# Sparse attention in a two-block transformer kernel: other places for weight splits, PSUM temporaries, and another order of attention units

## The chip, the cores and the metric

The kernel runs on one core of a Trainium2 chip. The time is the device time of one execution in microseconds (us); lower is better. The engines are TensorE (PE, with PEld for its weight loads), VectorE (DVE), ScalarE (ACT) and GpSimd (POOL); SyncE (SP) issues the weight DMAs. Each engine runs its instructions in program order.

## The reference

Two transformer blocks on 256 tokens of width 1024. The first has a convolution and neighbourhood attention, then a mixture of 16 experts. The second has sparse attention (DSA), an MLP, latent attention (MLA) and another MLP. The change lies in the sparse attention:

```python
score = einsum('bqh,bqhs->bqs', wib * 8**-0.5, relu(einsum('bqhd,bsd->bqhs', qib, ki) * 64**-0.5))
score = where(admiss, score, NEG)
_, idx = lax.top_k(score, n_top)              # n_top = 64 of up to 256 keys
logits = q . k[idx] * 64**-0.5 + bias[idx]    # 16 heads of 64; q and k RMS-normalised
out = (softmax(where(valid, logits, NEG)) @ v[idx]) @ w_o
```

## The kernel before, in words

The program is written in a manual order: each engine takes its instructions in the order in which the Python code emits them. Weights come by DMA from SyncE through a ring of buffers (`take`, `free`, `pump`); a buffer is loaded again when both halves in it have been freed.

*Splits.* The large products of this part run as three fp32r matmuls (`mm3`: high·high, low·high, high·low). Each 128x2048 weight tile is split by `split`: ScalarE copies the high half (L330), then VectorE (L334) or GpSimd (L332) subtracts to get the low half. The splits are numbered: 0 to 3 are the projections of k, index q, index k and v (`kvi`), 4 to 7 the four q projections (`qproj`), 8 to 11 the output projection (`WO.slot`), 12 and on the MLP. The set `on_dve` (L1092) says which low halves are VectorE's; the others are GpSimd's. `wahead(k)` emits the splits up to number k - 1 where it stands in the program, and `wnext(la)` hands out the next one after emitting `la` more ahead.

*Index.* For two tiles of 128 queries (qt = 0, 1; tile 1 sees 256 keys, tile 0 sees 128) `index_mm` makes the scores of 8 heads, `index_acc` accumulates them with per-row weights on VectorE (L1386, L1388, L1390), and `index_top` finds the 64 largest by 8 rounds of max and match-replace (L1398, L1399) and writes a mask (L1400). Before that, the row scales `rr` come from column sums by a chain of small VectorE instructions, the last eight of them in `rsq` (L288 to L295, a reciprocal square root from an integer guess and two refinements), and are broadcast by TensorE into a PSUM bank `rb_`.

*Query scales.* `qstat` sums the squares of q on TensorE, and `qscale(g)` turns the sums of 8 heads into scales, again by `rsq`.

*Attention.* It works on 8 units (qt, u) of 4 heads. `pipeline` emits for i = -2, -1, 0, ...: the scores S(i+2) (`dsa_score`, two PSUM banks of tag A, the mask added by a matmul with `idr`), the finished output fin(i-2) (`hilo_v`, L346 and L347), the normalisation of unit i (reciprocals L1254 on VectorE, the product L1255 on GpSimd), the softmax of unit i+1 (`dsa_soft`: sums L1479 and negated maxima L1482 on VectorE, exponentials L1484 on ScalarE), the functions in `pre[i]`, the values PV(i-1), the transposes T(i) (L1265, copied by ScalarE, L1268), and the functions in `hooks[i]`. In the call, the first dictionary is `hooks`, the second `pre`.

Four PSUM banks of tag A and four of tag B go round; a bank is written again when its last reader is done.

## Time and profile before

| | us |
|---|---|
| median of 3 runs | 1748.01 (1747.1 to 1751.78) |
| profiled execution, device time | 1741.9 |
| its span, first to last instruction | 1740.1 |

| engine | busy us | share of the span | instructions |
|---|---|---|---|
| PE | 1356.5 | 78% | 9581 |
| PEld | 873.8 | 50% | 9581 |
| DVE | 542.5 | 31% | 1037 |
| ACT | 426.0 | 24% | 649 |
| POOL | 271.8 | 16% | 124 |

The shares are averages over stages: up to about 1110 us the experts' weights stream in, and the chain of waits is DMA; from there on it is engines. The index and the sparse attention lie between about 1150 and 1251 us. The mean granted TensorE clock is 0.885. In timeline rows, a start and a length in us stand in front, and brackets at the end give the idle time before the instruction and what ended it.

### The profile page before, as it was taken

How to read it: one execution, taken by the hardware profiler on the slowest of the kernel's cores; microseconds unless marked ns; L12 is line 12 of the kernel's file. 1: busy time of each engine (PE TensorE's matmuls, PEld its weight loads, DVE VectorE, ACT ScalarE, POOL GpSimd, SP SyncE). 2: the span in 40 equal slices, each digit the busy share in tenths (PEclk: the TensorE clock that was granted, in tenths of full speed). 3: DMA queues.
4: the chain of work that ended last, by engine and by line, in shares of the span. 5: the costliest groups of instructions: out<-in, count | busy, mean ns of one | idle time of the engine just before them, and what ended most of it. 6: DMA issues, size and time to landing. Idle time of an engine off the chain costs nothing.

```text
span 1740.1 us, 22284 instructions
## 1 busy us (share of the span) xinstructions
PE 1356.5 (78%) x9581; PEld 873.8 (50%) x9581; DVE 542.5 (31%) x1037; ACT 426.0 (24%) x649; POOL 271.8 (16%) x124
## 2 busy tenths in 40 slices
PE   6899987666666655665666656798999999999998
PEld 3775842111111111221111111385899999889998
DVE  3885321000000000000000000278653457756434
ACT  3434510000000000000000000254554446455442
POOL 2521210000000000000000000152335221323531
PEclk9999999868778878878788787798999999999999
DMA  9649779999999999999999999972255544225450
GB/s 397 240 156 417 290 326 429 427 428 428 427 428 428 427 428 427 427 429 427 428 427 428 428 428 428 399 287 97 97 194 194 194 174 154 97 98 194 178 201 34
DMA packets 59475, 545.85 MB, mean 314 GB/s; under 512 B 5552, under 2 KB 9008, under 8 KB 26032
## 3 DMA queue, kind: packets, MB, share of 16 engines
q1 hardware_dynamic: 56400, 537.71, 74.9%
q10 hardware_dynamic: 2976, 6.72, 1.1%
q8 instruction: 75, 1.23, 0.3%
q14 instruction: 24, 0.20, 0.0%
HBM read 543.36 MB, written 1.05 MB: 313 GB/s over the span
## 4 chain that ended last, share of the span: by engine, by line
DMA 52%; PE 38%; DVE 5%; ACT 3%; issue 2%; POOL 1%; ACTq 0%; SPq 0%; DVEq 0%; POOLq 0%
DMA moe__w<-in_w_gu_dram 32%; DMA moe__w<-in_w_dn_dram 15%; PE mlp__psB L94 10%; PE mlp__psA L94 9%; PE index__psA L94 2%; DMA moe__w<-in_w_dl_dram 2%; PE mlaproj__psA L94 1%; PE mlawo__psA L94 1%; PE qkv__psA L94 1%; PE qkv__psB L94 1%; PE uproj__psA L94 1%; PE moe__psB L94 1%; DMA na__nb<-in_nab_dram 1%; PE router__psB L94 1%; PE wout__psA L94 1%
## 5 line engine op out<-in xcount | busy, mean ns | idle before, releaser
L94 PE MATMUL moe__psB<-moe__w,moe__xsT 128*32 128x512 f32 x1920 | 304.0, 767 | 191.7 <-DMA moe__w<-in_w_gu_dram 191.6
L94 PEld LDWEIGHTS moe__psB<-moe__w,moe__xsT 128*32 128x32 f32 x1920 | 58.9, 126 | 422.9 <-DMA moe__w<-in_w_gu_dram 312.3
L94 PE MATMUL moe__psB<-moe__w,moe__hT 128*32 128x512 f32 (+1 forms) x984 | 167.5, 808 | 103.1 <-DMA moe__w<-in_w_dn_dram 94.1
L1134 DVE TENSOR_TENSOR moe__hid<-moe__hid,moe__psB 128x512 f32<-128x512 f32 x15 | 10.3, 687 | 555.8 <-PE moe__psB L94 555.8
L332 POOL TENSOR_TENSOR dsaproj__wl<-moe__w,dsaproj__wh 128x1680 fp32r<-128x1680 f32 (+1 forms) x5 | 19.7, 3945 | 908.9 <-ACT dsaproj__wh L330 902.2
L94 PEld LDWEIGHTS moe__psB<-moe__w,moe__hT 128*32 128x32 f32 x984 | 38.4, 133 | 214.9 <-DMA moe__w<-in_w_dn_dram 139.7
L94 PE MATMUL mlp__psA<-mlp__hh,mlp__wl 128*128 128x256 f32 x512 | 141.3, 276 | 0.0
L94 PE MATMUL mlp__psA<-mlp__hh,mlp__wh 128*128 128x256 f32 x512 | 141.3, 276 | 0.0
L94 PE MATMUL mlp__psA<-mlp__hl,mlp__wh 128*128 128x256 f32 x512 | 141.3, 276 | 0.0
L1133 ACT ACTIVATE moe__hid<-moe__psB 128x512 f32<-128x512 f32 x15 | 9.0, 597 | 537.8 <-PE moe__psB L94 537.8
L94 PE MATMUL mlp__psB<-mlp__xgh,mlp__wh 128*128 128x256 f32 x448 | 123.8, 276 | 0.0
L94 PE MATMUL mlp__psB<-mlp__xgh,mlp__wl 128*128 128x256 f32 x448 | 123.7, 276 | 0.0
L94 PE MATMUL mlp__psB<-mlp__xgl,mlp__wh 128*128 128x256 f32 x448 | 123.7, 276 | 0.0
L330 ACT ACTIVATE mlp__wh<-mlp__w 128x2048 fp32r<-128x2048 f32 (+1 forms) x51 | 96.8, 1900 | 62.3 <-PE mlp__psA L94 48.6
L334 DVE TENSOR_TENSOR mlp__wl<-mlp__w,mlp__wh 128x2048 fp32r<-128x2048 f32 (+1 forms) x35 | 84.7, 2420 | 80.1 <-ACT mlp__wh L330 80.1
L332 POOL TENSOR_TENSOR mlp__wl<-mlp__w,mlp__wh 128x2048 fp32r<-128x2048 f32 x16 | 74.4, 4648 | 147.5 <-ACT mlp__wh L330 147.5
L94 PEld LDWEIGHTS mlp__psA<-mlp__hh,mlp__wh 128*128 128x128 f32 x512 | 96.1, 188 | 0.0
L94 PEld LDWEIGHTS mlp__psA<-mlp__hl,mlp__wh 128*128 128x128 f32 x512 | 96.1, 188 | 0.0
L94 PEld LDWEIGHTS mlp__psA<-mlp__hh,mlp__wl 128*128 128x128 f32 x512 | 96.1, 188 | 0.0
L1169 DVE COPY moe__ys<-moe__psB 128x512 f32<-128x512 f32 x15 | 10.4, 691 | 243.7 <-PE moe__psB L94 243.7
L94 PEld LDWEIGHTS mlp__psB<-mlp__xgh,mlp__wl 128*128 128x128 f32 x448 | 84.1, 188 | 0.0
L94 PEld LDWEIGHTS mlp__psB<-mlp__xgl,mlp__wh 128*128 128x128 f32 x448 | 84.1, 188 | 0.0
(602 smaller groups left out, 2508.2 us busy)
## 6 DMA issues: line engine op xcount, KB each, us to landing
moe__w<-in_w_gu_dram SPq DMA_DIRECT2D x120, 2048.0 KB, 39.1
moe__w<-in_w_dn_dram SPq DMA_DIRECT2D x57, 2048.0 KB, 39.1
mlp__w<-in_mlp_down_dram SPq DMA_DIRECT2D x28, 1024.0 KB, 7.0
mlp__w<-in_mlp_up_dram SPq DMA_DIRECT2D x20, 1024.0 KB, 4.9
qkv__w<-in_w_mod_dram SPq DMA_DIRECT2D x12, 1024.0 KB, 7.0
start__w<-in_w_mod_dram SPq DMA_DIRECT2D x8, 1024.0 KB, 13.5
mod__w<-in_w_gu_dram SPq DMA_DIRECT2D x4, 2048.0 KB, 20.8
wout__w<-in_w_gu_dram SPq DMA_DIRECT2D x4, 2048.0 KB, 8.4
```

The costliest lines, as they stand in the source:

```text
L94: nc.tensor.matmul(o, lhsT, rhs, start=start, stop=stop, skip_group_check=True)
L330: nc.scalar.activation(h[:, 0:n], f, AF.Copy)
L332: nc.gpsimd.tensor_tensor(out=l[:, 0:n], in0=f, in1=h[:, 0:n].bitcast(F32), op=ALU.subtract)
L334: nc.vector.tensor_tensor(out=l[:, 0:n], in0=f, in1=h[:, 0:n].bitcast(F32), op=ALU.subtract)
L1133: nc.scalar.activation(hid, gp, AF.Silu)
L1134: nc.vector.tensor_mul(hid, hid, up)
L1169: nc.vector.tensor_copy(ys[1], yp[1])
```

## The change

The low halves of splits 7 and 9 go from GpSimd to VectorE. Split 5 moves from the end of `kvi` to a place in front of the accumulation of query tile 1; split 6 from in front of the first q projection to behind it; split 7 to behind the accumulation of tile 0; splits 8 and 9 from in front of the attention into it (`pre[2]`, `pre[3]`). A new helper `rsq_p` keeps half of its temporaries, and its input, in PSUM. The row sums, their products and the query sums stay in their PSUM banks. The accumulation of tile 1 reads the broadcast scale from PSUM. The identity's cast goes from GpSimd to ScalarE. The softmax adds and takes its maxima in the score bank, and the exponentials read that bank. The units' order is new, and the second top-k (`itop`) stands one hook behind the second query scale instead of in front of it.

```diff
+    def rsq_p(pool_, v, n, tag, ps):
+        r, r1, out_ = (small(pool_, n, tag + k) for k in "012")
+        t = small(pool_, n, "rq_t")
+        a, b = ps[:, 0:n], ps[:, n:2 * n]
+        nc.vector.tensor_scalar(r.bitcast(I32), v.bitcast(I32), -0.5, 1597463007.0, ALU.mult, ALU.add)
+        nc.vector.tensor_tensor(out=a, in0=v, in1=r, op=ALU.mult)
+        nc.vector.tensor_tensor(out=t, in0=a, in1=r, op=ALU.mult)
+        nc.vector.scalar_tensor_tensor(out=b, in0=t, scalar=-10.0 / 3.0, in1=t, op0=ALU.add, op1=ALU.mult)
+        nc.vector.scalar_tensor_tensor(out=r1, in0=b, scalar=5.0, in1=r, op0=ALU.add, op1=ALU.mult)
+        nc.vector.scalar_tensor_tensor(out=a, in0=v, scalar=-27.0 / 1024.0, in1=r1, op0=ALU.mult, op1=ALU.mult)
+        nc.vector.tensor_tensor(out=b, in0=a, in1=r1, op=ALU.mult)
+        nc.vector.scalar_tensor_tensor(out=out_, in0=b, scalar=0.5625, in1=r1, op0=ALU.add, op1=ALU.mult)
+        return out_
...
-        on_dve = {5, 8, 10, 11} | {n for n in range(12, 90) if n % 3 or 43 < n < 54}
+        on_dve = {5, 7, 8, 9, 10, 11} | {n for n in range(12, 90) if n % 3 or 43 < n < 54}
...
-                w = wnext(2 if s == 3 else 0)
+                w = wnext(1 if s == 3 else 0)
...
-        vr = cols[:, 0:4]
-        v1, pv, iv1, v2c, ep, ipv = (cols[:, 2 * i:2 * i + 2] for i in range(6))
+        v1, iv1, ep = (cols[:, 2 * i:2 * i + 2] for i in range(3))
+        vr = sps[:, 32:36]
+        vp1, pv, v2c, ipv = (sps[:, 32 + 2 * i:34 + 2 * i] for i in range(4))
...
-        nc.gpsimd.tensor_copy(idr, ident)
...
+        nc.vector.tensor_scalar(vp1, sps[:, 0:2], 1.0 / D, EPS, ALU.mult, ALU.add)
...
-        rr = rsq(pa, vr, 4, "rr")
+        rr = rsq_p(pa, vr, 4, "rr", sps[:, 64:72])
...
         def qproj(u):
-            w = wnext()
+            w = wnext(0)
...
-            vq = small(pool_, 16, "vq")
+            vq = qc[:, 32:48]
...
-            rqq = rsq(pool_, vq, 16, "rqq")
+            rqq = rsq_p(pool_, vq, 16, "rqq", qc[:, 64:96])
...
-            nc.vector.tensor_tensor(out=sc[:, 0:nk], in0=sc[:, 0:nk], in1=r12b[:, 0:nk], op=ALU.mult)
+            nc.vector.tensor_tensor(out=sc[:, 0:nk], in0=sc[:, 0:nk], in1=r12[:, 0:nk], op=ALU.mult)
...
-        rk = rsq(pa, vk, 2, "rk")
-        scs[1] = index_acc(1, rl1)
+        rk = rsq_p(pa, vk, 2, "rk", kst[:, 16:20])
+        wahead(6)
+        scs[1] = index_acc(1, rl1, rb_)
         rl0 = index_mm(0)
         nc.scalar.activation(r1b, rb_[:, T:2 * T], AF.Copy)
+        nc.scalar.activation(idr, ident, AF.Copy)
         qproj(0)
+        wahead(7)
         index_top(1, scs[1])
...
-        scs[0] = index_acc(0, rl0)
+        scs[0] = index_acc(0, rl0, r12b)
+        wahead(8)
         qproj(1)
         qstat(0)
         qproj(2)
         qstat(1)
-        wahead(10)
...
+                psv = pss[par][:, 0:2 * nk].rearrange("p (a k) -> p a k", a=2)
...
-                    nc.vector.scalar_tensor_tensor(out=s[:, a, 0:nk], in0=pss[par][:, a * nk:(a + 1) * nk],
-                                                   scalar=rq[:, qt, hd:hd + 1], in1=bm[:, 2 * par + a, :],
-                                                   op0=ALU.mult, op1=ALU.add)
-                nc.vector.tensor_reduce(nmx, s[:, :, 0:nk], axis=AX.X, op=ALU.max, negate=True)
+                    nc.vector.scalar_tensor_tensor(out=psv[:, a, :], in0=psv[:, a, :], scalar=rq[:, qt, hd:hd + 1],
+                                                   in1=bm[:, 2 * par + a, :], op0=ALU.mult, op1=ALU.add)
+                nc.vector.tensor_reduce(nmx, psv, axis=AX.X, op=ALU.max, negate=True)
...
-                    nc.scalar.activation(s[:, a, 0:nk], s[:, a, 0:nk], AF.Exp, bias=nmx[:, a:a + 1],
+                    nc.scalar.activation(s[:, a, 0:nk], psv[:, a, :], AF.Exp, bias=nmx[:, a:a + 1],
...
-                  [(1, 0), (1, 1), (1, 2), (0, 0), (0, 1), (1, 3), (0, 2), (0, 3)])
+                  [(1, 0), (1, 1), (1, 2), (1, 3), (0, 0), (0, 1), (0, 2), (0, 3)])
...
-        pipeline(att, 8, "dsaatt", {-2: [lambda: qscale(0, pb)], -1: [q_last, itop], 0: [q_last2], 8: [wo.slot(2, (1,))]},
-                 {6: [wo.slot(0), x3(range(0, 3))], 7: [wo.slot(1), x3(range(3, 6))],
+        pipeline(att, 8, "dsaatt", {-2: [lambda: qscale(0, pb)], -1: [q_last], 0: [q_last2], 1: [itop], 8: [wo.slot(2, (1,))]},
+                 {2: [lambda: wahead(9)], 3: [lambda: wahead(10)], 6: [wo.slot(0), x3(range(0, 3))], 7: [wo.slot(1), x3(range(3, 6))],
```

## Rows read from the trace of the kernel before

**Rows 1.** Chain of waits, 1149 to 1256 us: start us, us, what.

```profile
1173.71 5.66 PE index__psA L94 x48
...
1189.81 8.05 PE index__psA L94 x48
...
1198.81 1.73 PE dsaatt__psA L94 x10
...
1224.28 6.11 PE dsawo__psA L94 x48
...
1231.40 0.60 PE dsaatt__psB L1265 x4
```

**Rows 2.** Windows: engines' busy us (xcount), granted TensorE clock, DMA share, GB/s.

```profile
1188.80:1205.50 16.70, 14.95 (x94) 11.85 (x94) 13.96 (x55) 6.56 (x20) 2.04 (x2) 0.82 0.30 122
1205.50:1224.00 18.50, 15.41 (x97) 10.04 (x97) 16.20 (x51) 12.55 (x45) 8.48 (x10) 0.86 0.00 1
1224.00:1251.00 27.00, 26.80 (x219) 24.65 (x217) 15.88 (x31) 12.28 (x20) 9.11 (x5) 0.97 0.25 84
```

**Rows 3.** VectorE timeline, 1149 to 1181: start us, us, instruction, [idle before, releaser].

```profile
1149.68 4.97 DVE L334 TENSOR_TENSOR dsaproj__wl<-moe__w,dsaproj__wh 128x2048 fp32r<-128x2048 f32 x1 [3.18 <-ACT dsaproj__wh L330]
...
1159.77 0.35 DVE L1386 TENSOR_SCALAR index__sc<-index__rl,dsaproj__wi 128x256 f32<-128x256 f32 x1
...
1172.62 1.95 DVE L1400 TENSOR_SCALAR dsaproj__msk<-index__sc 128x256 fp32r<-128x256 f32 x1
...
1180.39 0.41 DVE L1351 COPY dsaatt__rw<-index__psB 8x256 f32<-8x256 f32 x1
```

**Rows 4.** GpSimd timeline, 1147 to 1188 us.

```profile
1147.92 4.58 POOL L332 TENSOR_TENSOR dsaproj__wl<-moe__w,dsaproj__wh 128x2048 fp32r<-128x2048 f32 x1 [3.44 <-PE dsaproj__psB L94]
...
1169.83 4.59 POOL L332 TENSOR_TENSOR index__wl<-dsaproj__w,index__wh 128x2048 fp32r<-128x2048 f32 x1 [0.84 <-ACT index__wh L330]
...
1182.54 4.51 POOL L332 TENSOR_TENSOR index__wl<-dsaproj__w,index__wh 128x2048 fp32r<-128x2048 f32 x1 [8.12 <-ACT index__wh L330]
```

**Rows 5.** TensorE timeline, the broadcast of the row scales.

```profile
1157.14 2.00 PE L94 MATMUL index__psA<-cst,dsaproj__rr 128*128 128x128 f32 x8 [3.52 <-DVE dsaproj__rr L295]
```

**Rows 6.** ScalarE timeline, 1159 to 1230 us.

```profile
1159.18 0.38 ACT L1416 ACTIVATE dsaproj__r12b<-index__psA 128x256 f32<-128x256 f32 x1 [5.13 <-PE index__psA L94]
...
1191.32 0.19 ACT L1484 ACTIVATION_READ_ACCUMULATOR dsaatt__ss<-dsaatt__ss,dsaatt__nmx 128x1 f32 x1
...
1198.52 0.63 ACT L1338 ACTIVATE index__sq<-dsaproj__qs 128x512 f32<-128x512 f32 x1
...
1227.51 1.90 ACT L330 ACTIVATE dsawo__wh<-dsaproj__w 128x2048 fp32r<-128x2048 f32 x1
```

**Rows 7.** VectorE timeline, 1182 to 1206 us.

```profile
1182.70 4.37 DVE L288 TENSOR_SCALAR dsaatt__rqq<-dsaatt__vq 128x16 int32<-128x16 int32 x1
...
1188.78 0.88 DVE L1479 SCALAR_TENSOR_TENSOR dsaatt__ss<-dsaatt__psA,dsaproj__rq,dsaproj__t 128x256 f32<-128x256 f32 x2
...
1197.72 0.23 DVE L1400 TENSOR_SCALAR dsaproj__msk<-index__sc 128x128 fp32r<-128x128 f32 x1
...
1202.41 0.41 DVE L1351 COPY index__rw<-index__psB 8x256 f32<-8x256 f32 x1 [1.33 <-PE index__psB L94]
...
1205.49 0.86 DVE L1479 SCALAR_TENSOR_TENSOR dsaatt__ss<-dsaatt__psA,dsaproj__rq,dsaproj__t 128x256 f32<-128x256 f32 x2
```

**Rows 8.** VectorE timeline, 1208 to 1233 us.

```profile
1208.50 0.42 DVE L346 CAST index__mixah<-dsaatt__psB 128x256 fp32r<-128x256 f32 x1
...
1224.34 0.59 DVE L1479 SCALAR_TENSOR_TENSOR dsaatt__ss<-dsaatt__psA,dsaproj__rq,dsaproj__t 128x128 f32<-128x128 f32 x2
...
1229.45 2.29 DVE L334 TENSOR_TENSOR dsawo__wl<-dsaproj__w,dsawo__wh 128x2048 fp32r<-128x2048 f32 x1 [3.09 <-ACT dsawo__wh L330]
...
1231.65 1.27 DVE L1503 SCALAR_TENSOR_TENSOR x<-x,vec,dsaproj__r1b 128x256 f32<-128x256 f32 x3
```

**Rows 9.** VectorE group by line and shape, whole span: busy us, mean ns.

```profile
L670 DVE SCALAR_TENSOR_TENSOR conv__psA<-rms__vp,vec,conv__psA 128x256 f32<-128x256 f32 x120 | 58.8, 490 | 4.1
```

More of the change, by code (lines that the diff above doesn't have):

```diff
@@ L1379, in index_mm, with index_acc @@
             return rls
-        def index_acc(qt, rls):
+        def index_acc(qt, rls, r12):
             nk = P * (qt + 1)
@@ L1416 @@
         nc.scalar.activation(r12b, rb_[:, 0:T], AF.Copy)
-        vk = small(pa, 2, "vk")
+        vk = kst[:, 8:10]
         nc.vector.scalar_tensor_tensor(out=vk, in0=kst[:, 0:2], scalar=1.0 / 64, in1=ep, op0=ALU.mult, op1=ALU.add)
-        rk = rsq(pa, vk, 2, "rk")
-        scs[1] = index_acc(1, rl1)
+        rk = rsq_p(pa, vk, 2, "rk", kst[:, 16:20])
+        wahead(6)
+        scs[1] = index_acc(1, rl1, rb_)
         rl0 = index_mm(0)
         nc.scalar.activation(r1b, rb_[:, T:2 * T], AF.Copy)
+        nc.scalar.activation(idr, ident, AF.Copy)
         qproj(0)
+        wahead(7)
         index_top(1, scs[1])
```

## The prediction

> **What bounds the kernel now.** I read the chain of waits first, then the windows, then the timelines of single engines. The chain shows that from 1149 to 1251 us several engines take turns in setting the end: the q projections on TensorE (5.66 us for 48 matmuls, but 8.05 us for the last one), a score block (1.73 us), then the output projection from 1224.28 us [rows 1]. The windows split this stretch. From 1205.5 to 1224 us VectorE is busy for 16.20 of 18.5 us: the attention loop is VectorE's. From 1224 to 1251 us TensorE is busy for 26.80 of 27 us, and the MLP follows on TensorE, so whatever moves the first output-projection slot (1224.28) moves the end by as much [rows 1, 2]. The question is therefore when VectorE lets that slot start. I follow VectorE from the index to there in four parts, A to D, and work out each part's length after the change.
>
> **A. Up to the first softmax (now 1188.78 us).**
> The low half of split 5 (4.97 us) stands ahead of the row-scale chain and leaves it [rows 3]. The scales then start up to 4.97 us earlier. But TensorE is only free for their broadcast 3.52 us before it starts now, at 1153.6 [rows 5], and split 5 comes back ahead of the accumulation: VectorE waits there for ScalarE's high half, which stands behind the copy of the broadcast. Broadcast at 1153.6; the copy follows its start by 2.04 us and takes 0.38 [rows 5, 6], so 1156.0; high half 1.90 us [rows 6]; low half 2.29 us [rows 8]. That is 1160.2, against an accumulation that starts at 1159.77 now [rows 3]. If the broadcast runs in half its 2.00 us, 1159.2. I take 0, bounds -0.6 to +0.5. The eight top-k rounds are not touched.
> The mask instruction takes 1.95 us because GpSimd's subtraction runs from 1169.83 to 1174.42 and the mask ends just after; the same instruction at half the width takes 0.23 us with GpSimd idle [rows 3, 4, 7]. GpSimd now has only split 6 here, and 7 goes to VectorE in the place that split 8 has now (2.3 us each, no difference). The mask gives back 1.6 us (bounds 1.5 to 1.7).
> The first query scale takes 8.39 us from its copy at 1180.39 to the softmax at 1188.78; the second, of the same instructions, takes 2.95 us (1202.41 to the reciprocals before 1205.49) [rows 3, 7]. Of the difference, 4.2 us is one integer tensor_scalar of 4.37 us that ends when GpSimd's split 9 does (1182.54 + 4.51) [rows 4, 7]; the rest is a wait for TensorE's score blocks, which are done earlier now. Split 9 is gone from there and the operands lie in PSUM. That gives 5.3 us; the least is 4.2.
> A = 0 - 1.6 - 5.3 = **-6.9 us** (-7.6 to -5.2); first softmax at 1181.9.
>
> A place for the Trainium skill. The page "SBUF — State Buffer", section "Who interferes with whom", says that a VectorE instruction contends with GpSimd if it runs in a two-port mode or has two inputs in SBUF, and not if one of two inputs is in PSUM. The rows above agree with the stalls (4.97 and 4.37 us beside 4.58 and 4.51 us of GpSimd). By that rule one instruction of the new helper is still held: (t - 10/3)·t reads SBUF twice while GpSimd's split 4 runs until 1152.5. It would put the broadcast some 0.4 us later and the sum at +13.4 instead of +13.0; no row here shows it.
>
> **B. First to third softmax (now 1188.78 to 1205.49, 16.71 us).**
> The softmax now works in its PSUM bank, so a bank comes free after ScalarE's exponentials and no longer after VectorE's sums. The last q projection waits for such a bank: it now starts 1.03 us after the softmax (1189.81) [rows 1, 7]; the exponentials of that half end 2.73 us after it (1191.51) [rows 6]: +1.7 us. It took 8.05 us instead of 5.66 after a wait, in a window with a mean granted clock of 0.82 [rows 1, 2]; its wait gets shorter, since the softmax comes sooner after the score blocks, so I take 7.4, nearer to 8.05 (-0.65; bounds 0 and -2.4). The third score block now starts 0.95 us after it (1198.81). After the change it needs the second unit's exponentials, which stand on ScalarE behind the projection's copy and square; the square ends 1.3 us after the projection [rows 1, 6], one half's exponentials take 1.2 (2.73 less half of a softmax's 3.01): 2.5 instead of 0.95, +1.5 us. From there to the third softmax nothing changes. VectorE is through with two softmaxes some 7 us after the first begins and has nothing until the second scale's copy, some 16 us after it: the second top-k, which fills this gap now (it ends at 1197.95, as the projection does [rows 1, 7]), has been taken out of it.
> B = 1.7 - 0.65 + 1.5 = **+2.5 us** (0 to +3.2).
>
> **C. Third softmax to the first slot (now 1205.49 to 1224.28, 18.8 us).**
> Terms: a wide softmax 3.01 us (1205.49 to 1208.50), a narrow one 2.0 (1224.34 to 1229.45 less 3.09), the split of a finished unit's output 0.84 (two instructions of 0.42), the reciprocals 0.2 [rows 7, 8]. The second top-k takes 6.16 us (1188.78 + 3.01 to 1197.95) [rows 7]. Splits 8 and 9 are asked for right behind a softmax, as split 10 is now: its low half waits 3.09 us, because its high half stands on ScalarE behind that softmax's exponentials, then takes 2.29 [rows 8]. VectorE's queue is in order, so behind each wait stand the output split, the reciprocals and the next softmax, and GpSimd, TensorE and ScalarE wait for these.
> VectorE's list after the change: softmax 3.01, top-k 6.16, output and reciprocals 1.04, softmax 3.01, split 5.38; 1.04, 2.0, split 5.38; 1.04, 2.0; 1.24, 2.0; and the output of unit 4, which the first slot now needs, 0.84. Sum 34.1 us, against 18.8 now, which had the same five softmaxes.
> C = **+15.3 us**. Lower bound: if both high halves were ready without a wait, +9.1. Upper: exponentials of a wide unit are longer, and a stall of TensorE ahead of the slot, +17.
> The softmax itself in PSUM: a scalar_tensor_tensor into PSUM has a mean of 490 ns [rows 9], one into SBUF about 440 (a pair in 0.88) [rows 7]. That is at most 0.05 us each, under 1 us in this part; I bound the reduction in the same way. It may be less than nothing, since ScalarE then reads PSUM instead of SBUF; taken at 0.
>
> **D. From the first slot on.**
> The second slot now follows at 1232.0, 7.7 us after the first, behind unit 6's transposes [rows 1]. After the change it needs unit 5, whose output split comes after 0.3 + 2.0 (reciprocals, softmax) + 3.09 + 2.29 (split 10) + 1.27 (scaling of x) + 0.84 = 9.8 us [rows 8]. D = **+2.1 us** (0 to +3.5). The rest of the projection has the same order as now.
>
> Small edits cost nothing as long as VectorE sets the pace: the identity's cast on ScalarE (idle for 5.13 us before the copy [rows 6]), one more scale column, split 6 behind the first q projection (TensorE waits about 1 us for it, beside VectorE's second accumulation). If VectorE did not set it, that wait is what they cost. Two pairs of MLP weights are loaded only when split 9 releases its buffer, some 40 us later; they are first used after the output projection, so nothing waits.
>
> **Sum.** -6.9 + 2.5 + 15.3 + 2.1 = +13.0 us. The profiled execution took 1741.9 us, so 1754.9 in a like one. The other runs lie at 1747.1 to 1751.8, median 1748.0, 6 us above the profiled one; I put the same difference on the median: **1761.0 us**.
>
> **Rivals.**
> *The added work is hidden (no change).* If the top-k lay beside another wait and both splits found their high halves ready, C would be 15.3 - 6.2 - 6.2 = 2.9 and the sum +0.6: 1748.6. For it: VectorE is free for 2.3 us of the 18.5, and ScalarE is busy for only 12.55 [rows 2]. Against it: 2.3 us holds neither, and split 10's wait shows the same queue at work.
> *Faster: VectorE is not what the first slot waits for.* Place: the attention loop, whose chain also holds TensorE blocks. If the loop is as long as now with the added work inside it, C and D are 0, and with the last q projection at full clock (5.66) B is +0.8: -6.1, so 1741.9. It decides at C + D below about 1 us. For it: TensorE is busy for 15.41 of 18.5 us in the same window, nearly as much as VectorE [rows 2]. Against it: the list of C is 34 us of one in-order queue.
> *Slower still.* TensorE gets three new waits (before the fifth score block, the first and the second slot), and it has come back from a wait slowly: 8.05 instead of 5.66 us [rows 1]. At 2.4 us for each of the two slots the sum is +17.8: 1765.8.
> That the splits don't move is no rival: every engine runs its program order.
>
> **How the numbers follow.** Chances: forecast 0.60, slower still 0.18, hidden 0.13, faster 0.09. From no change a measurement tells about 0.3%, 5.2 us. The forecast and the slower case lie above that but for a small part, so slower 0.77; hidden gives most of same, 0.13; faster 0.10. The bounds of the parts add up to +1.5 (-7.6 + 0 + 9.1 + 0) and +18.5 (-5.2 + 3.2 + 17 + 3.5), 1749.5 and 1766.5; the range is 1748 to 1768, which leaves out the faster case and half of the hidden one.
>
> **What would show it.** Right: the first query scale in about 3 us and the mask in under 0.5; VectorE idle for 5 us or more before the second scale's copy; two waits of about 3 us before the low halves of splits 8 and 9; the first output slot 30 us or more after the third softmax. A is wrong if the first softmax doesn't come 5 to 8 us earlier against the start of the row scales' stage. The forecast is wrong if the first slot follows the third softmax in under 25 us, or if the second top-k stands beside the last q projection after all.

## The result and the profile after

The changed kernel takes 1766.09 us (median of 4 runs, 1762.18 to 1769.59) against 1747.6 us for the kernel before in the same session: a ratio of 1.0095, 95% interval 1.0066 to 1.0125. It is slower, as forecast; the forecast of 1761.0 us was 5.1 us too low, and the time lies inside the range. Two of the four runs took 1762 us and two 1769.6 us; the profile is of one of the shorter, and no profile shows where the longer ones lose 7 us more. The profiled execution took 1762.61 us with a span of 1760.8 us, 20.7 us more than the profiled one of before.

I measure every profile with one ruler: from the start of VectorE's last pair of instructions at L459 (L445 before), which gives the index its input, to the first matmul of the MLP. Before, this stretch takes 107.64 us (1143.25 to 1250.89); after, 122.76 us (1143.66 to 1266.42). So 15.1 us of the 20.7 are lost around the change. Upstream the two differ by 0.4 us; the other 5.2 us are lost behind it, 3.8 of them in the MLP, and have another cause, which stays open (below).

The chain of waits of the changed kernel, from the index to the output projection (start us, us, what); rows of before: [rows 1].

```profile
1172.63 5.50 PE index__psA L94 x46
...
1185.35 1.28 ACT L1502
...
1187.72 7.46 PE index__psA L94 x48
...
1196.14 1.72 PE dsaatt__psA L94 x10
...
1199.73 0.42 DVE index__rw L1366
...
1212.50 0.80 PE dsaatt__psA L94 x2
...
1217.78 1.81 ACT dsaatt__wh L344
1219.61 2.29 DVE dsaatt__wl L348
...
1225.96 1.81 ACT dsaatt__wh L344
1227.79 2.29 DVE dsaatt__wl L348
...
1243.23 2.29 DVE dsawo__wl L348
...
1247.56 5.61 PE dsawo__psA L94 x47
```

The reader is to see two things. Between the third softmax (1203 us) and the first output slot (1237.89 us) both splits are on the chain, each with its ScalarE half and its VectorE half. And between the first softmax and the last projection stands a piece without a tile name, 1.28 us of ScalarE: the load of the table for the exponential, which no part of the prediction had.

The windows of the same three stretches as in [rows 2]: first to third softmax, third softmax to the first slot, the slots.

```profile
1183.50:1203.00 19.50, 14.78 (x94) 11.40 (x94) 9.29 (x29) 7.34 (x21) 2.04 (x2) 0.82 0.11 44
1203.00:1238.20 35.20, 23.99 (x105) 14.66 (x102) 27.33 (x81) 15.92 (x49) 8.48 (x10) 0.58 0.16 60
1238.20:1266.90 28.70, 27.29 (x215) 24.33 (x213) 16.00 (x30) 11.66 (x17) 6.97 (x5) 0.98 0.23 78
```

In the first stretch VectorE now works for 9.29 us where it worked for 13.96: it stands idle. In the second it works for 27.33 of 35.20 us, and the stretch is nearly twice as long. TensorE is busy for 23.99 us of it, and its mean granted clock is 0.58, against 0.86 before.

VectorE's timeline, the instructions that the prediction's steps turn on.

```profile
1151.48 1.44 DVE L305 SCALAR_TENSOR_TENSOR dsaproj__psA<-dsaproj__rq_t 128x4 f32<-128x4 f32 x1
...
1181.08 0.50 DVE L1372 TENSOR_SCALAR dsaatt__psB<-dsaatt__psB,dsaproj__cols 128x8 f32<-128x8 f32 x2 [1.53 <-PE dsaatt__psB L1369]
...
1199.73 0.41 DVE L1366 COPY index__rw<-index__psB 8x256 f32<-8x256 f32 x1 [7.66 <-PE index__psB L94]
...
1212.21 0.23 DVE L1415 TENSOR_SCALAR dsaproj__msk<-index__sc 128x128 fp32r<-128x128 f32 x1
...
1219.61 2.29 DVE L348 TENSOR_TENSOR dsaatt__wl<-dsaproj__w,dsaatt__wh 128x2048 fp32r<-128x2048 f32 x1 [2.94 <-ACT dsaatt__wh L344]
...
1227.79 2.29 DVE L348 TENSOR_TENSOR dsaatt__wl<-dsaproj__w,dsaatt__wh 128x2048 fp32r<-128x2048 f32 x1 [2.73 <-ACT dsaatt__wh L344]
```

The idle time that the second top-k used to fill is there (7.66 us before the second query scale's copy; 1.33 before [rows 7]). So are the two waits of about 3 us before the low halves of splits 8 and 9.

GpSimd, ScalarE and TensorE of the changed kernel: what held L305, the waits that the prediction did not have or sized otherwise, and the first exponential of the second unit.

```profile
1148.34 4.56 POOL L346 TENSOR_TENSOR dsaproj__wl<-moe__w,dsaproj__wh 128x2048 fp32r<-128x2048 f32 x1 [3.44 <-PE dsaproj__psB L94]
...
1164.43 0.38 ACT L1438 ACTIVATE dsaproj__r1b<-index__psA 128x256 f32<-128x256 f32 x1 [2.97 <-DVE index__sc L1405]
...
1172.63 0.39 PE L94 MATMUL index__psA<-moe__xgh,index__wl 128*128 128x256 f32 x1 [2.98 <-POOL index__wl L346]
...
1185.35 1.28 ACT L1502 ACT_TABLE_LOAD   x1 [5.92 <-DVE dsaatt__nmx L1500]
...
1187.72 0.58 PE L94 MATMUL index__psA<-moe__xgh,index__wh 128*128 128x256 f32 x1 [4.96 <-ACT dsaatt__ss L1502]
...
1196.38 0.46 ACT L1502 ACTIVATE dsaatt__ss<-dsaatt__psA,dsaatt__nmx 128x256 f32<-128x256 f32 x1
...
1212.50 0.80 PE L94 MATMUL dsaatt__psA<-dsaproj__msk,dsaproj__idr 128*128 128x256 f32 x2 [4.30 <-DVE dsaproj__msk L1415]
...
1247.10 0.39 PE L94 MATMUL dsawo__psA<-index__mixah,dsaatt__wh 128*128 128x256 f32 x1 [0.81 <-DVE index__mixah L360]
```

The longest wait of TensorE in the loop is that of the fifth score block, the first of query tile 0: it stands still for 4.30 us until the moved top-k has written that tile's mask.

In the kernel before, the table load ran long before the first exponential, in ScalarE's idle time:

```profile
1182.48 1.28 ACT L1484 ACT_TABLE_LOAD   x1
...
1190.41 0.51 ACT L1484 ACTIVATE dsaatt__ss<-dsaatt__ss,dsaatt__nmx 128x256 f32<-128x256 f32 x1 [6.65 <-DVE dsaatt__nmx L1482]
```

What is lost behind the change. The same 90 us of the MLP, both at a granted clock of 1.00 (2.4 GHz), in the kernel before:

```profile
1275.00:1365.00 90.00, 89.46 (x790) 89.40 (x790) 39.96 (x34) 44.08 (x42) 40.51 (x13) 1.00 0.48 181
```

and in the kernel after:

```profile
1275.00:1365.00 90.00, 90.00 (x767) 90.00 (x766) 38.94 (x33) 44.18 (x46) 40.66 (x13) 1.00 0.51 188
```

TensorE is busy all the time in both, but it issues a matmul every 0.1132 us (89.46/790) in one and every 0.1173 us (90.00/767) in the other. Of all twelve profiles in this study the slower pace shows in three: this one and those of the second and third experiment. The runs e5, e6 and e8 have the whole of the changed kernel's loop and the faster pace, so the loop's change alone does not set the pace. What does is open; there is one profile for each kernel, so whether it differs between runs of one kernel is not shown. It makes about 4 us between one profile and another, and I therefore read the experiments by the stretch above and not by their medians alone.

### The profile page after: what moved, and what is told of

Same layout as the page of the kernel before. It is cut to its first block, busy times and chain, and to the rows that moved or that the text cites. A ratio compares the mean times of both kernels' runs of the same rounds, so it can differ in the third digit from the quotient of the medians.

```text
span 1760.8 us, 22295 instructions
## 1 busy us (share of the span) xinstructions
PE 1365.9 (78%) x9581; PEld 883.7 (50%) x9581; DVE 541.8 (31%) x1040; ACT 424.9 (24%) x650; POOL 257.8 (15%) x121
## 4 chain that ended last, share of the span: by engine, by line
DMA 51%; PE 38%; DVE 5%; ACT 3%; issue 2%; POOL 1%; ACTq 0%; SPq 0%; DVEq 0%; POOLq 0%
DMA moe__w<-in_w_gu_dram 31%; DMA moe__w<-in_w_dn_dram 15%; PE mlp__psB L94 11%; PE mlp__psA L94 9%; PE mlaproj__psA L94 2%; DMA moe__w<-in_w_dl_dram 2%; PE mlawo__psA L94 1%; PE qkv__psA L94 1%; PE qkv__psB L94 1%; PE uproj__psA L94 1%; DMA na__nb<-in_nab_dram 1%; PE moe__psB L94 1%; PE router__psB L94 1%; PE dsaproj__psB L94 1%; PE wout__psA L94 1%
## 5 line engine op out<-in xcount | busy, mean ns | idle before, releaser
L94 PE MATMUL moe__psB<-moe__w,moe__xsT 128*32 128x512 f32 x1920 | 296.0, 750 | 192.3 <-DMA moe__w<-in_w_gu_dram 192.0
L94 PEld LDWEIGHTS mlp__psB<-mlp__xgh,mlp__wh 128*128 128x128 f32 x448 | 84.1, 188 | 0.0
```

The costliest lines, as they stand in the source:

```text
L94: nc.tensor.matmul(o, lhsT, rhs, start=start, stop=stop, skip_group_check=True)
```

## The experiments

The theory: VectorE runs its list in order, and this list sets the first output slot; whatever is put into it behind the third softmax costs its own length and its wait. The rival: other engines set the loop, and the added work lies beside their waits. The table gives each profile's parts: from the L459 pair to the first softmax, from there to the first matmul of the output projection, from there to the first matmul of the MLP, and the sum (us). The last column is the ratio of the times to the kernel before, with its 95% interval. The expectations of e1 to e4 count the stretch to the MLP's second matmul, 0.5 us later (108.1 us before, 123.2 after).

| Run | to 1st softmax | to 1st slot | to MLP | sum | ratio of times |
|---|---|---|---|---|---|
| before | 45.53 | 35.15 | 26.96 | 107.64 | 1 |
| after | 39.86 | 54.37 | 28.53 | 122.76 | 1.0095 (1.0066–1.0125) |
| e1, top-k back | 42.64 | 49.29 | 28.52 | 120.45 | 1.0066 (1.0034–1.0098) |
| e2, splits back | 41.23 | 45.20 | 28.84 | 115.27 | 1.0058 (1.0030–1.0085) |
| e3, softmax in SBUF | 41.47 | 49.08 | 30.08 | 120.63 | 1.0079 (1.0044–1.0114) |
| e4, all three and the order back | 44.37 | 34.51 | 32.11 | 110.99 | 1.0017 (0.9992–1.0042) |
| e5, table early | 42.48 | 52.82 | 28.53 | 123.83 | 1.0070 (1.0045–1.0095) |
| e6, r1 copy early | 38.43 | 55.42 | 28.52 | 122.37 | 1.0059 (1.0034–1.0085) |
| e7, first part alone | 40.74 | 36.03 | 26.53 | 103.30 | 0.9962 (0.9942–0.9983) |
| e8, filler | 41.77 | 55.41 | 28.53 | 125.71 | 1.0068 (1.0045–1.0091) |
| e9, e7 and square from PSUM | 40.54 | 36.67 | 26.80 | 104.01 | 0.9971 (0.9956–0.9986) |
| e10, before and PSUM softmax | 45.51 | 41.59 | 27.54 | 114.64 | 1.0045 (1.0023–1.0067) |

**e1_itop_back.** The second top-k stands behind the last projection again.

```diff
-{-2: [lambda: qscale(0, pb)], -1: [q_last], 0: [q_last2], 1: [itop], 8: ...}
+{-2: [lambda: qscale(0, pb)], -1: [q_last, itop], 0: [q_last2], 8: ...}
```

> The changed kernel with one part undone: the second top-k is issued after the last query projection again, ahead of the second softmax. Read by the stretch from the x2 row of the expert layer (L445) to the first matmul of the MLP, which was 108.1 us before and 123.2 us after. Theory (VectorE's list in order sets the first output slot): the 6.2 us top-k falls into the 7.7 us that VectorE waits for the last projection, so the stretch is 6 us shorter, 117 us (116 to 118), and VectorE's wait before the second query scale shrinks to under 2.5 us. Rival (the slot is set by the waits of the two splits and by the other engines, and the top-k lies beside them): the stretch loses 0 to 2 us, 121 to 123, and the idle time comes back before the low halves 8 and 9.

Measured: the sum fell by 2.3 us only, to 120.45, between the windows of theory and rival. The parts say why. The first softmax, ahead of which nothing was changed, came 2.78 us later than in the profile of the changed kernel; from there to the first slot it took 49.29 us for 54.37, so 5.1 us less (from the third softmax to the slot alone 29.15 us for 34.90, 5.75 less). VectorE's wait before the second query scale:

```profile
1204.68 0.41 DVE L1366 COPY index__rw<-index__psB 8x256 f32<-8x256 f32 x1 [3.98 <-PE index__psB L94]
```

The top-k fills the gap, but 3.98 us are left and not under 2.5, since the last projection took longer too (46.84 to 54.97 us after the pair: 8.1 us for 7.46). The theory holds with 5.1 of its 6 us. Where the first 2.78 us come from was a new question; e6 and e8 answer it.

**e2_splits_early.** Splits 8 and 9 are asked ahead of the last projection.

```diff
-... -1: [q_last], 0: [q_last2] ...   {2: [lambda: wahead(9)], 3: [lambda: wahead(10)], 6: ...}
+... -1: [lambda: wahead(10), q_last], 0: [q_last2] ...   {6: ...}
```

> The changed kernel with another part undone: splits 8 and 9 are asked ahead of the last query projection instead of inside units 3 and 4 of the attention. Theory (each of the two costs its 2.29 us and a wait for ScalarE of 2.7 to 2.9 us in VectorE's order, and before the last projection VectorE has nothing else to do): the stretch from the x2 row to the first MLP matmul falls by 10 us, from 123.2 to 113 us (112 to 115). Rival (only the instructions themselves count, the waits would be filled by something else that is late, the values of earlier units): it falls by 4.6 us or less, 118.6 or more.

Measured: from the first softmax to the first slot 45.20 us for 54.37, 9.2 us less, twice the rival's 4.6. The sum is 115.27, just above the theory's window, again because the first softmax came later (41.23). The low halves now stand in the gap; what is left of it:

```profile
1205.42 0.41 DVE L1366 COPY index__rw<-index__psB 8x256 f32<-8x256 f32 x1 [1.27 <-PE index__psB L94]
```

So the waits count too: of the 10.25 us of the two splits (2.94 + 2.29 and 2.73 + 2.29) 9.2 come back, about 4.6 us a split, 2.29 us of work and the rest standing behind ScalarE's exponentials.

**e3_softmax_sbuf.** The scores go to SBUF again.

```diff
-scalar_tensor_tensor(out=psv[:, a, :], in0=psv[:, a, :], ...)
+scalar_tensor_tensor(out=s[:, a, 0:nk], in0=pss[par][:, a * nk:(a + 1) * nk], ...)
-activation(s[:, a, 0:nk], psv[:, a, :], AF.Exp, ...)
+activation(s[:, a, 0:nk], s[:, a, 0:nk], AF.Exp, ...)
```

> The changed kernel with its third part undone: the softmax's scores are written to SBUF again and not over their PSUM bank. Theory: the bank comes free 3 us sooner, the load of the exponential's table goes back in front of the wait (1.3 us), so the last projection starts 1.5 us rather than 4.2 us after the first softmax; and 32 scalar_tensor_tensor and 16 maximum instructions of the softmaxes are shorter (0.44 for 0.51 us the wide ones), 1.4 us up to the first slot: the stretch is 118.7 us (117.5 to 120) against 123.2. Rival (the last projection waits for its weights or VectorE's own list is so late that neither counts): 122 to 124.

Measured: from the first softmax to the first slot 49.08 us for 54.37, 5.3 less. The sum, 120.63, is above the theory's window because both ends are longer (41.47 and 30.08 us; the granted clock in the slots is 0.93 for 0.98). The table load runs without a wait, 4.1 us ahead of the softmax at 1186.93:

```profile
1182.84 1.28 ACT L1502 ACT_TABLE_LOAD   x1
```

and the last projection waits for VectorE's sums and no longer for ScalarE, 1.02 us behind the softmax instead of 4.20:

```profile
1187.95 0.36 PE L94 MATMUL index__psA<-moe__xgh,index__wh 128*128 128x256 f32 x1 [1.79 <-DVE dsaatt__ss L1497]
```

Up to the third softmax this gives back 3.3 us (16.15 for 19.47), and 2.0 us in the loop behind it. The rival falls.

**e4_old_attention.** All that the change did behind the first softmax is undone, the order of the units too; split 8 is asked after the third projection and split 9 with the first slot.

```diff
+        wahead(9)            # behind qproj(2)
-                    self.w = wnext()
+                    self.w = wnext(1 if self.stg == "dsawo" and s < 2 else 2)
-[(1, 0), (1, 1), (1, 2), (1, 3), (0, 0), (0, 1), (0, 2), (0, 3)]
+[(1, 0), (1, 1), (1, 2), (0, 0), (0, 1), (1, 3), (0, 2), (0, 3)]
```

> Only the first part of the change, that on the index up to the first softmax; behind it the attention is as before (softmax in SBUF, the top-k and the units in the old order), split 8 is asked after the third query projection and split 9 with the first output slot. Theory (the first part gained 5.7 us, and all else lost): the stretch is 102.6 us (101.5 to 104.5) against 108.1 before and 123.2 after, and the whole time 5 us under the kernel before, if the MLP behind it keeps its pace. Rival (what was gained before the first softmax is given back, since the last projection and the splits 8 and 9 are not sooner): 106.5 to 109, the time of before.

Measured: 110.99 us, a miss of both. The first softmax is late (44.37), since the low half of split 8, 2.3 us, now stands on VectorE ahead of the first query scale. From the first softmax to the first slot it takes 34.51 us, 19.9 less than after; the three single undoings add up to 5.1 + 9.2 + 5.3 = 19.6. The cost of the loop is thus accounted for; if the costs add up as they seem to, the order of the units is worth next to nothing, but no run changed it alone. But the way I placed the splits lost 5.2 us in the slots (32.11 for 26.96):

```profile
1241.36 4.87 POOL L346 TENSOR_TENSOR dsawo__wl<-index__w,dsawo__wh 128x2048 fp32r<-128x2048 f32 x1 [8.22 <-ACT dsawo__wh L344]
...
1241.73 5.17 DVE L1522 SCALAR_TENSOR_TENSOR x<-x,vec,dsaproj__r1b 128x256 f32<-128x256 f32 x2
...
1247.38 0.55 PE L94 MATMUL dsawo__psA<-index__mixah,dsawo__wh 128*128 128x256 f32 x1 [3.50 <-DVE index__mixah L360]
```

VectorE's scaling of x (three of them take 1.27 us in [rows 8]) met GpSimd's subtraction of split 12, and two took 5.17 us, the first of them until GpSimd was done (1246.23); the last unit's output stood behind them, and TensorE waited 3.50 us.

**e5_early_table.** One more Exp of a single column on ScalarE, ahead of the first softmax.

```diff
+        def early_exp():
+            dm = small(pb, 1, "dm", 1)
+            nc.scalar.activation(dm, ep[:, 0:1], AF.Exp)
-{-2: [lambda: qscale(0, pb)],
+{-2: [early_exp, lambda: qscale(0, pb)],
```

> The changed kernel with one more instruction: an Exp of one column on ScalarE, whose result nobody reads, issued ahead of the first softmax's wait. In the changed kernel the load of the exponential's table (1.28 us) stands between the first softmax's maximum and its first Exp. Theory (the load is on the path from the first softmax to the last query projection): the projection starts 2.9 us after the first softmax (2.7 to 3.1) instead of 4.2, and the way from the first softmax to the first output slot falls from 54.4 us by up to 1.3. Rival (the projection waits for something else, its weights or the second bank, or the load comes where it was since ScalarE is late): it still starts 4.0 to 4.3 after the first softmax.

Measured:

```profile
1184.49 1.28 ACT L1467 ACT_TABLE_LOAD   x1
...
1191.50 0.58 PE L94 MATMUL index__psA<-moe__xgh,index__wh 128*128 128x256 f32 x1 [3.67 <-ACT dsaatt__ss L1506]
```

The first softmax starts at 1188.58 (42.48 after the pair), so the projection starts 2.92 us behind it: the theory's 2.9. From the softmax to the slot it takes 52.82 us, 1.55 less, a little over the 1.3 of the theory. Of the 3.2 us by which the PSUM softmax puts the projection off, 1.3 are the table and 1.9 are the exponentials that read the bank.

**e6_r1b_early.** ScalarE's copy of r1 stands right behind that of r12.

```diff
         nc.scalar.activation(r12b, rb_[:, 0:T], AF.Copy)
+        nc.scalar.activation(r1b, rb_[:, T:2 * T], AF.Copy)
...
-        nc.scalar.activation(r1b, rb_[:, T:2 * T], AF.Copy)
```

> The changed kernel with ScalarE's copy of r1 out of the broadcast's bank moved up, right behind the copy of r12, so that it does not wait for VectorE's reading of the same bank (2.97 us), and the copies and the split behind it come sooner. Theory 1 (this wait delays split 6, and split 6 the third query projection): TensorE's 2.98 us wait for GpSimd's part of split 6 goes to under 1.3 us and the third projection starts 1.5 to 3 us sooner than the 29.0 us after the x2 row that it has in five profiles. Theory 2 (this idle time is also why the granted clock of that projection fell to 0.58 to 0.79 in four of those five profiles): the clock from 29 to 36 us after the x2 row is 0.95 or more, and the first softmax starts at 37 to 39 us, against 39.9 (clock 1.00) and 41.2 to 44.4 (the others). Rival (ScalarE's order is filled otherwise, split 6 waits for its buffer): third projection at 28.5 to 29.0, clock as it falls.

Measured:

```profile
1165.12 4.60 POOL L346 TENSOR_TENSOR index__wl<-dsaproj__w,index__wh 128x2048 fp32r<-128x2048 f32 x1 [12.42 <-ACT index__wh L344]
...
1169.77 0.38 PE L94 MATMUL index__psA<-moe__xgh,index__wl 128*128 128x256 f32 x1 [0.34 <-POOL index__wl L346]
```

The third projection starts 26.3 us after the pair (1169.77 less 1143.45) instead of 29.0, TensorE waits 0.34 us instead of 2.98, and the first softmax comes at 38.43. Both theories hold for this part. But the sum is only 0.4 us shorter: the last projection took 8.53 us for 7.46, and the loop behind it is as long as ever.

**e8_filler.** Twelve small matmuls into unused columns, where TensorE waits ahead of the third projection.

```diff
         qstat(0)
+        for _ in range(12):
+            mm(qrow[0][0:8, T:2 * T], selk(0, 8), sq2[0][:, 0, :], False, False)
         qproj(2)
```

> The changed kernel with twelve more matmuls of 8 x 256 behind the first two of the query statistics, into columns of a bank that nobody reads, so that TensorE is busy for some 2.6 of the 2.98 us in which it waits for GpSimd's part of split 6. Nothing else starts sooner. Theory (the granted clock of the third query projection falls because TensorE stood still ahead of it): the clock from 29 to 36 us after the x2 row is 0.95 or more (0.58 to 0.79 in four of five profiles without the filler), and the first softmax starts at 39.5 to 40.5 us. Rival (the clock falls for other reasons, the load of the whole stage): clock 0.58 to 0.85, first softmax at 41 to 45 us.

Measured: the windows from 29 to 36 us after the pair, in which the third projection runs. The number behind GpSimd's busy time is the granted clock. In the run e1, without the filler:

```profile
1174.16:1181.16 7.00, 7.00 (x37) 7.00 (x38) 5.65 (x12) 0.00 (x0) 0.00 (x0) 0.58 0.00 0
```

with the filler:

```profile
1171.56:1178.56 7.00, 7.00 (x55) 5.89 (x54) 5.64 (x12) 0.00 (x0) 0.00 (x0) 1.00 0.00 0
```

and in e6, without the wait:

```profile
1172.45:1179.45 7.00, 6.03 (x44) 4.38 (x44) 6.24 (x15) 1.23 (x2) 0.00 (x0) 1.00 0.00 0
```

Six profiles have the wait of 2.98 us and no filler: after, e1 to e5. In five of them the granted clock of this window is 0.58, 0.79, 0.76, 0.80 and 0.60, so TensorE ran at its lower level of 1.2 GHz for part of it and the 48 matmuls took up to 2.8 us longer; only the profile of the changed kernel itself kept 1.00. In the four profiles in which the pause is filled or at most 0.54 us long (e6, e7, e8, e9) it is 1.00, and so it is in before and e10, which have no pause there. So the clock falls only behind the pause of TensorE in front of the projection, mostly but not each time; with one profile for each kernel this is a strong sign and not a proof. The first softmax did not come at 39.5 to 40.5 us but at 41.77, since the fillers were longer than the pause and the projection began 1.7 us late (30.65 for 28.97): a filler that overruns costs as much as the clock it saves.

**e7_first_part.** The first part of the change, with the early copy; everything behind the first softmax as before.

```diff
-on_dve = {5, 7, 8, 9, 10, 11}
+on_dve = {5, 7, 8, 10, 11}
         qproj(2)
+        wahead(9)
-... -1: [q_last], 0: [q_last2], 1: [itop] ...
+... -1: [lambda: wahead(10), q_last, itop], 0: [q_last2] ...
```

(and the edits of e3, of e6 and of the units' order in e4)

> The first part of the change alone, with what the runs so far showed: the copy of r1 moved up, softmax in SBUF, old order of the units, the second top-k behind the last projection, split 8 asked after the third query projection and split 9 ahead of the last one with its low half on GpSimd; the output slots ask for their splits as before, so that GpSimd's low half does not meet the two-input instructions of VectorE in slot 2. Theory: first softmax at 38 to 41 us after the x2 row (45.5 before), 34.5 us from there to the first slot (35.2 before), 27 us from the slot to the MLP (27.0 before): 100 to 102.5 us in all against 107.6 before, a time 5 to 7 us under the kernel before (ratio 0.996 to 0.997). Rival (the clock that falls after a pause of TensorE takes it back, or the slots wait again as in the run before): 106 us or more, ratio 0.999 to 1.002.

Measured: 1741.06 us (median of 12 runs, 1737.43 to 1745.15) against 1745.86 (21 runs), a ratio of 0.9962 (0.9942 to 0.9983): 0.4% faster than the kernel before. The stretch is 103.30 us, 0.8 above the theory's window. One term was wrong: 36.03 us from the softmax to the slot, not 34.5. Its chain shows the place.

```profile
1198.04 1.83 DVE dsaproj__msk L1415
...
1225.48 5.86 PE dsawo__psA L94 x48
...
1252.13 3.91 PE mlp__psB L94 x32
```

The second mask takes 1.83 us instead of 0.23 beside GpSimd's subtraction of split 9, the stall that the first mask had before [rows 3, 4]. I had moved it and not removed it. This mask has one input, in SBUF; so not only two-input instructions are held, while the top-k rounds beside the same subtraction kept their length.

**e9_psum_square.** In e7, the square's two inputs are one in SBUF and one in PSUM.

```diff
+        c = ps[:, 2 * n:3 * n]
+        nc.vector.tensor_tensor(out=c, in0=a, in1=r, op=ALU.mult)
-        ...scalar_tensor_tensor(out=b, in0=t, scalar=-10.0 / 3.0, in1=t, ...)
+        ...scalar_tensor_tensor(out=b, in0=c, scalar=-10.0 / 3.0, in1=t, ...)
```

> The first part of the change alone (the run that was faster than before), and in it one more edit: of the instruction (t - 10/3) t of the inverse square root, which took 1.43 us for 128x4 because both its inputs lie in SBUF while GpSimd works on the low half of split 4, one input is read from PSUM, where a second multiplication puts the same t. Theory (an instruction of VectorE with one input in SBUF is not held by GpSimd): it takes 0.2 us, the added one 0.2, so the first query projection starts about 1.0 us sooner, at 11.7 us after the x2 row for 12.8 in nine profiles, and the stretch to the MLP is 0 to 1.0 us shorter than in the run before (103.3), if the clock does the same. Rival (the instruction waits for something else that ends at the same time, the ScalarE copy or the weights): it takes 1.2 us or more again, and the projection starts at 12.8 to 13.0.

Measured:

```profile
1150.03 0.17 DVE L307 SCALAR_TENSOR_TENSOR dsaproj__psA<-dsaproj__psA,dsaproj__rq_t 128x4 f32<-128x4 f32 x1
```

The instruction takes 0.17 us instead of 1.43, as the theory said, but the first projection starts at 12.48 us and not at 11.7: TensorE is busy for 12.00 of the 12 us from 10 us after the pair on, and it was for 11.80 in e7, so nearly all that was left there was its own work, the scores and transposes. The sum (104.01) and the time (0.9971, 0.9956 to 0.9986) are not to be told from e7's.

**e10_psum_softmax.** The kernel before with the softmax of the change alone (the edit of e3 the other way round).

> The kernel before with only the third part of the change: the softmax's scores are written over their PSUM bank. Theory (the price that the undoing showed, 5.3 us, holds in the kernel before as well, since there too the last projection waits for the bank): the last projection starts 4.2 us after the first softmax for 1.0 before (46.56 less 45.53), 3.2 us later, and the softmaxes cost 1.4 us more up to the first slot: the stretch from the x2 row to the MLP is 111.5 us (110.5 to 113) for 107.6. Rival (only the later release of the bank counts, 1.7 us as the prediction had it, and the slower instructions lie beside other engines): 108 to 109.8.

Measured: 114.64 us, 7.0 more than before and above both windows; the time is 1.0045 (1.0023 to 1.0067) of before. The last projection starts 4.19 us behind the softmax, as expected, behind the same load:

```profile
1190.92 1.28 ACT L1484 ACT_TABLE_LOAD   x1 [8.14 <-DVE dsaatt__nmx L1482]
```

Up to the third softmax that costs 3.2 us. Another 3.2 us (21.64 for 18.44) are lost from there to the slot, of which I had expected 1.4. TensorE shows why:

```profile
1213.55 1.22 PE L94 MATMUL dsaatt__psA<-dsaproj__kk,dsaproj__qs 64*128 64x128 f32 x6 [1.02 <-ACT dsaatt__ss L1484]
...
1225.78 0.49 PE L94 MATMUL dsaatt__psA<-dsaproj__kk,dsaproj__qs 64*128 64x128 f32 x2 [1.04 <-ACT dsaatt__ss L1484]
1227.44 0.71 PE L94 MATMUL dsaatt__psA<-dsaproj__kk,dsaproj__qs 64*128 64x128 f32 x6 [1.17 <-ACT dsaatt__ss L1484]
```

Three score blocks wait over 1 us each for the exponentials that still read their bank. In the kernel before, one block of scores has such a wait, of 0.23 us, and for VectorE.

## Why the prediction was right, and where it was not

The direction was right because the bound was: the first output slot waits for VectorE's list. Undoing the two things that were put into it took 5.1 and 9.2 us off (e1, e2), 14.3 us, where the prediction had 15.3 for C. The top-k also costs through TensorE, whose fifth score block waits 4.30 us for its mask; how much of its 5.1 us goes that way no run separates.

**A, up to the first softmax: predicted -6.9, measured -5.7 in the profile after, and -2.9 to -4.3 in e1, e2, e3 and e5, which have the same work there.** The mask (0.29 us) and the free query scale came as forecast; but the scale still waits 1.53 us for TensorE, and the whole way from its copy to the softmax is 4.4 us, not 3.1, so that 4.0 of its 5.3 us came. The step that failed is the one put among the small edits, that split 6 makes TensorE wait about 1 us at no cost. That "about 1 us" came from no row. It waits 2.98 us, because ScalarE's copy of r1 was held until VectorE had read the other half of the same bank, and split 6 stands behind that copy. Behind that pause the clock of the third projection falls in most profiles. e6 takes the wait away and gets 38.43 us, -7.1.

The prediction named the Trainium skill's page "SBUF — State Buffer", section "Who interferes with whom", by which a two-input instruction of VectorE with both inputs in SBUF contends with GpSimd, and one with an input in PSUM does not. The trace agrees on both sides: L305 took 1.44 us, until GpSimd's split 4 ended at 1152.90, and 0.17 us with one input in PSUM (e9). The instruction lost 1.3 us; of the 0.4 us by which the prediction saw the broadcast late for it, 0.21 us stand in the trace as TensorE's wait, and when e9 took the hold away 0.3 us came back.

**B, first to third softmax: predicted +2.5, measured +2.8, by other terms.** The last projection took 7.46 us (7.4 forecast). It starts 3.2 us later behind the softmax and not 1.7: the bank's release is 1.9 of it, and 1.3 is the table load, which the prediction left out, since in the kernel before it lies in idle time of ScalarE and is on no chain (e3, e5). The third score block was not delayed by 1.5 us at all. It starts 0.96 us behind the projection, at 1196.14, before the second unit's exponentials begin (1196.38), so it does not wait for their banks; by the order of the code the free ones are those of the first unit's second half and of the projection. Two errors of about 1.5 us cancelled: that B came out right is luck.

**C, third softmax to the first slot: predicted +15.3, measured +16.5** (34.90 us from the third softmax to the first matmul of the slot, for 18.44). The top-k (6.2 us) and the two splits, with waits of 2.94 and 2.73 us for 3.09, are as forecast. The softmax in PSUM, taken at 0 with a bound of 1 us, costs 2.0 us here by e3. Most of it is longer instructions: the ten pairs of the five softmaxes take some 0.13 to 0.14 us more each (1.01 us for 0.88 the wide ones, 0.73 for 0.59 the narrow), 1.4 us in all. The rest fits the bank, which is held until the exponentials are through, but that was not measured here.

**D, from the first slot on: predicted +2.1, measured +1.6** (28.53 for 26.96). The second slot waits for unit 5's output (0.81 us of TensorE's idle time), behind split 10's wait of 2.74 us, as said.

**The sum.** Predicted +13.0, measured +15.1 in the stretch, inside the bounds of +1.5 to +18.5; 15.1 us are a ratio of 1.0086, inside the measured interval. The rest of the 20.7 us between the two profiles lies outside the stretch, most of it in the pace of the matmuls in the MLP, which no step had; e5, e6 and e8, with the changed kernel's loop, have the faster pace. The rival of hidden work is out, since both waits were there; the faster one too. "Slower still" named three new waits of TensorE: the one ahead of the fifth score block is 4.30 us, the one ahead of the second slot 0.81 us and not 2.4, and ahead of the first slot the trace shows none.

What stays open: why the MLP runs at one pace or the other, and why the table load carries the softmax's wait when the exponential reads PSUM and not when it reads SBUF.

## What to carry to other kernels

Work that an in-order engine does in an idle stretch is free there and nowhere else: before moving it, find out what will fill the gap it leaves and what stands behind it at its new place, waits included. When a stage is overwritten in its PSUM bank, the bank's next user waits for the last reader: count what TensorE waits for there, and look where the table load went. Judge an edit by the stretch that it touches as well as by the whole time: here some 20 us of loss and 5.7 us of gain lay in one diff, and the gain, with r1's copy moved up, made the kernel 0.4% faster (e7).

## What the runs showed of the hardware

- At a granted clock of 1.00, the same stream of matmuls runs at 0.1132 us each in one profile and at 0.1173 in another, over 90 us (before and after); it makes about 4 us in this MLP (180.5 us to the next stage in the profile before, 184.3 in that after).
- A pause of TensorE of 2.98 us ahead of a block of 48 matmuls was followed by a granted clock of 0.58 to 0.80 over the next 7 us in five of six profiles, and by 1.00 in all six without it (at most 0.54 us, or filled). With the same code the first softmax came 39.9 to 42.6 us after the pair for that.
- ScalarE's read of a PSUM bank waited for VectorE's read of another part of it (2.97 us), though both only read; whether the chip asks for that or a semaphore of the program is not shown.
- Some one- and two-input instructions of VectorE from SBUF took as long as GpSimd's subtraction had still to run: a mask 1.83 us for 0.23, two scalings of x 5.17 us where three take 1.27. Top-k rounds beside the same subtraction took as long as without it (0.29 and 0.28 us in e7).
- A scalar_tensor_tensor of 128x256 that wrote its sum to PSUM took about 0.50 us for 0.44 into SBUF (pairs of 1.01 and 0.88), both with one input from PSUM.
